# Two-layer attention trunk on one core: a norm row loaded by broadcast, value products moved behind two blocks of filler work, one low part moved to VectorE

## The chip, the cores and the metric

The program runs on one core of a Trainium2 chip. The metric is device time in microseconds (us) of one execution. TensorE (PE) multiplies, VectorE (DVE), ScalarE (ACT) and GpSimd (POOL) do elementwise work, and nearly every DMA is issued by SyncE (SP) on one queue.

## The reference

Two layers over 512 tokens of width 1024, one sequence. Each layer:

```python
h = _rms(x, g_pre)
proj = h @ w_in
o_nsa = _nsa_attention(q_rope, q_nope, k_cmp, v_cmp, k_slc, v_slc, k_win, v_win, nsa_gate)
o_nsa = o_nsa * jax.nn.silu(p_nz)
o_gla = _rms(_gla(gq, gk, gv, log_a), gla_g_norm)
y = m_nsa * (o_nsa @ w_up_nsa) + m_gla * (o_gla @ w_up_gla)
out = y @ w_out
return x + _rms(out, g_post)
```

`_rms(x, g)` is `x * rsqrt(mean(x*x) + 1e-6) * g`. The NSA branch has 8 heads of 64 and adds three attentions (compressed blocks, selected blocks, a window), each with a softmax. With 512 tokens there are only 8 blocks of 64, so selection takes all of them, and both the selected and the window branch are causal attention over all earlier tokens with their own keys and values. The GLA branch is gated linear attention in chunks of 64.

## The kernel before

**Products.** A matrix product in full precision is made of three fp32r products: each operand is split into a high part H (a cast by ACT) and a low part Lo (a subtraction by DVE), and `split3` (lines 175 to 179) multiplies high by high, high by low, low by high. Weights come by DMA into `raw` tiles of which there are three, are split at lines 153 and 154 (or 147 and 148), and are then read by `fm` and `up`. `fm` and `up` are generators that yield after every three products.

**Order of work.** The order of PE's instructions is the order of the program, written by hand. In the first stage (`first_stage`) the order of the other engines is written out as well. Elsewhere a planner puts the instructions of ACT, DVE, POOL and SP in order at compile time, from its own estimates and from each one's place in the program; `tc.high_priority()` raises the instructions inside it. Each engine then runs its list strictly in order.

**First stage.** The x tile of 128 tokens comes in two halves of 512 columns, then A0 (the first weight tile of the first product). The two halves of the row `g_pre` (2 KB each) are loaded into one partition of zeroed tiles, and PE spreads each over 128 partitions by an fp32 product with ones (line 415) into PSUM. `scale_rows` (line 223) multiplies x by the row's factor and by this. `turn_half` transposes on PE, `high` and `low` (lines 241 and 245) make hT, and `prod` multiplies. `keep_busy` issues products on ones that nobody reads.

**Attention.** Heads go in four pairs p. A pair has five steps: m = 0 the compressed branch (`cmp_steps`), m = 1 to 4 `attn_steps` for (ip, br) = (0,0), (0,1), (1,0), (1,1). An attention step has two score units (`scores`: PE product, then DVE maximum at line 970, ACT exponential, DVE scale and transposition), after which SP writes the result to DRAM (line 940) and reads it back in another layout as four DMAs into `PT` (line 943). Its third part, called the values here, multiplies `PT` by v into the pair's accumulator `acc` (line 998). `acc` lies in the only PSUM buffer of tag "o"; the pair's third compressed part opens it (line 918). After a pair's last values, DVE reads it (line 1003, `f_`), ACT makes H (line 1005) and POOL the low part Lo (line 1006).

The loop of lines 1038 to 1061 weaves this: `go(n)` runs the next part of step n and `fill(us)` runs filler products (`fm` and `up` of the rest of the layer) worth that many us. So at m = 3 of pair p, `go(n - 5)` and `go(n - 4)` are the last values of pair p - 1 (ip = 1, both branches), and `go(n - 3)` opens pair p's `acc`:

```python
go(n)
if m == 3:
    go(n - 5)
    go(n - 4)
fill(f4[0])
```

The times of `FILL` for m = 3 are 1.5, 1.2, 1.5 and 1.8. After the loop the first 16 yields of the up products `un0` and `un1` run, then the last pair's last values, and then the rest: `un` multiplies weights by `oTn[0..3]`, which are the (H, Lo) of the four pairs, in `up`.

Of the kernel before, what the change touches and what calls it, by code (L numbers as in the profile page):

```python
# [9 lines left out]
F32 = mybir.dt.float32  # L10
# [4 lines left out]
OP = mybir.AluOpType  # L15
# [52 lines left out]
def trunk(ctx, tc, x, wpk, sp, gvec, cs, wa, out):  # L68
# [243 lines left out]
    for l in range(L):  # L312
# [73 lines left out]
        def first_stage():  # L386


            ones, rows = new("p", dt=BF), [new("p") for _ in range(2)]
            onef = new("p")[:, 0:128]  # L390
            for t in rows:
                V.memset(t, 0.0)
            V.memset(ones, 1.0)
            V.memset(onef, 1.0)
            idle = ps("o")

            def keep_busy(n):
                for _ in range(n):
                    mm(idle, ones[:, 0:128], ones, start=True, stop=True)

            xs = [[new("g") for _ in range(2)]]
            dma(xs[0][0], x[0:128, 0:512])
            nc.scalar.dma_start(xs[0][1], x[0:128, 512:1024])
            issue(0)
            for h in range(2):
                nc.scalar.dma_start(rows[h][0:1], gvec[0, 0:1, h * 512:(h + 1) * 512])
            for i in range(3):
                issue(i)
                xs.append(load_x(x, i + 1, "g"))
            dma(spt, sp[0])  # L410
            shapes = mask_shapes()
            keep_busy(WARM[0])
            gpre = [ps("s") for _ in range(2)]
            for h in range(2):
                mm(gpre[h], onef, rows[h], start=True, stop=True)
            xn = [[new("p") for _ in range(2)] for _ in range(2)]
            q2 = [new("sm", (128, 2), tag="q2") for _ in range(4)]
            xn += xn

            def split_w(n, part):  # L420
                r, w, H, Lo = first_w[n]
                if part:
                    V.tensor_sub(Lo[:, :w], r[:, :w], H[:, :w].bitcast(F32))
                else:
                    A.copy(H[:, :w], r[:, :w])

            acc = [ps("mm") for _ in range(3)]

            def prod(s, n, parts):

                for part in parts:
                    for k in range(n * 3, min(n * 3 + 3, KT)):
                        w = first_w[n][2 + part][:, (k % 3) * 296:(k % 3) * 296 + 296]
                        for t in hTs(k, s)[:2 - part]:
                            mm(acc[s][:, :296], t, w, start=(s, k, 0) not in begun and k == 0 and part == 0,
                               stop=(n == 2 and k == KT - 1 and part == 1))
                            begun.add((s, k, 0))

            begun = set()
            square(q2[0], xs[0], xn[0], 0, A)  # L440
            square(q2[0], xs[0], xn[0], 1, V)
            rs = row_scale(q2[0])
            split_w(0, 0)
            square(q2[1], xs[1], xn[1], 0, A)
            scale_rows(xs[0], xn[0], rs, gpre)
            keep_busy(WARM[1])
            b0 = [turn_half(xn[0], h) for h in range(2)]
            keep_busy(WARM[2])
            for h in range(2):
                high(0, h, b0[h], HT)  # L450
            square(q2[1], xs[1], xn[1], 1, V)
            rs = row_scale(q2[1])
            for h in range(2):
                low(0, h, b0[h], HT)
            split_w(1, 0)
            scale_rows(xs[1], xn[1], rs, gpre)
            prod(0, 0, (0,))
            prod(0, 1, (0,))
            b1 = [turn_half(xn[1], h) for h in range(2)]
            square(q2[2], xs[2], xn[2], 0, A)  # L460
            square(q2[2], xs[2], xn[2], 1, A)
            split_w(2, 0)
            split_w(0, 1)
            rs = row_scale(q2[2])
            for h in range(2):
                high(1, h, b1[h], HT)
                low(1, h, b1[h], HT)
            keep_busy(1)
            prod(0, 2, (0,))
            prod(0, 0, (1,))  # L470
            scale_rows(xs[2], xn[2], rs, gpre)
            for n in range(3):
                prod(1, n, (0,))
            prod(1, 0, (1,))
            b2 = [turn_half(xn[2], h) for h in range(2)]
            square(q2[3], xs[3], xn[3], 0, A)
            square(q2[3], xs[3], xn[3], 1, A)
            split_w(1, 1)
            rs = row_scale(q2[3])
            for h in range(2):  # L480
                high(2, h, b2[h], HT)
                low(2, h, b2[h], HT)
            prod(0, 1, (1,))
            prod(1, 1, (1,))
            scale_rows(xs[3], xn[3], rs, gpre)
            split_w(2, 1)
            drawn = masks(*shapes)
            for n in range(3):
                prod(2, n, (0,))
            for n in range(2):  # L490
                prod(2, n, (1,))
            b3 = [turn_half(xn[3], h) for h in range(2)]
            for h in range(2):
                a = high(3, h, b3[h], HT)
                v = low(3, h, b3[h], HT)
            behind.extend((a.ins, v.ins))
            for s in range(3):
                prod(s, 2, (1,))
                take_A(s, acc[s])
            acc.append(ps("o"))  # L500
            for n in range(3):
                prod(3, n, (0, 1))
            take_A(3, acc[3])
            return drawn
# [226 lines left out]
        def up(f, gate, wn, src, then):  # L731
            th = []

            def sig(o):
                th.append(new("th"))
                A.activation(th[0], o, AF.Tanh, scale=0.5)

            yield from fm(l, f"{gate}{f}", hT, sig)
            w = get(l, f"{wn}{f}")
            u = ps("mm")  # L740
            for k in range(4):
                sl = slice(k * 128, (k + 1) * 128)
                split3(u, (w[0][:, sl], w[1][:, sl]), src[k], k == 0, k == 3)
                if k == 3:
                    then(th[0], u)
                yield 0.64
# [233 lines left out]
        def attn_steps(p, ip, br):  # L980
            for i in (2 * ip, 2 * ip + 1):
                if i or not br:
                    scores(p, i, (br,) if i else (0, 1))
                else:
                    turn(p, br, i, held.pop(p))
                yield

            acc, W = PR[p][3], PT[p, br, ip]
            i0 = 2 * ip
            for j in range(i0 + 2):  # L990
                for g in range(2):
                    c0 = br * 128 + g * 64
                    if j <= i0:
                        m = W[:, :, :2 * (i0 + 1) * 64].rearrange("p a (i j g q) -> p i a j g q", i=2, g=2, q=32)
                        m, w = m[:, :, :, j, g], 256
                    else:
                        m, w = W[:, :, (2 * j) * 64 + g * 32:(2 * j) * 64 + g * 32 + 32], 128
                    mm(acc[g * 64:(g + 1) * 64, (i0 + 2) * 128 - w:(i0 + 2) * 128],  # L998
                       vsw[j // 2][:, j % 2, c0:c0 + 64], m,
                       start=False, stop=(br == 1 and j == i0 + 1), skip_group_check=True)  # L1000
            if ip == 1 and br == 1:
                f_ = new("p")
                V.scalar_tensor_tensor(f_, acc, 0.5, PR[p][2], op0=OP.mult, op1=OP.mult)
                H, Lo = new("oT", dt=F32R), new("oT", dt=F32R)
                A.copy(H, f_)  # L1005
                G.tensor_tensor(Lo, f_, H.bitcast(F32), op=OP.subtract)  # L1006
                oTn[p] = (H, Lo)
            yield

# [28 lines left out]
        for n in range(len(steps)):  # L1038
            m = n % 5
            f4 = FILL[m]  # L1040
            if m == 0:
                need(f"q{steps[n][0]}")
            if m == 4:
                need(f"nz{steps[n][0]}")
            go(n)
            if m == 3:
                go(n - 5)
                go(n - 4)
            fill(f4[0])
            if m == 2:  # L1050
                go(n - 2)
            fill(f4[1])
            if m != 0:
                go(n)
                fill(f4[2])
            if m == 3:
                go(n - 3)
            if m == 4:
                go(n - 3)
                go(n - 2)  # L1060
            fill(f4[3])
        need("ug7")

        uns = [up(f, "mgn", "un", oTn, take_un(f)) for f in range(8)]
# [123 lines left out]
```

## Time and profile before

| | |
|---|---|
| median of 3 runs | 809.79 us (808.65 to 813.39) |
| the profiled execution | 808.68 us |
| its span, first to last instruction | 807.0 us |
| PE busy | 789.5 us (98%) |
| DVE / ACT / POOL busy | 553.5 / 354.4 / 97.6 us |

In the rows an instruction is named by engine, line and operation. "[2.06 <-DMA PT<-tp]" behind a row says that the engine stood idle for 2.06 us before it and that this DMA ended the idle time, and x16 that 16 instructions are taken together. SPq rows are DMAs issued by SP. Busy times of PE are modelled, as matmuls are pipelined: starts are to be trusted more than ends.

### The profile page before, as it was taken

To read this page: it belongs to the slowest core of one execution; us is meant where nothing else is said; L and a number is where in the kernel's file an instruction comes from. 1 tells how busy PE (TensorE), PEld (TensorE's weight loads), DVE (VectorE), ACT (ScalarE), POOL (GpSimd) and SP (SyncE) were. 2 spreads that over 40 slices of the span, in tenths; PEclk is the share of its full clock that TensorE was granted. 3 is DMA by queue.
4 is the path that set the end of the run, shared out by engine and by line. 5 is a ranking of instruction groups with operands and counts; after the bars stand their busy time and mean duration, and the time that the engine had idled before them with its cause. 6 is when DMAs were issued, how large, how long until landed. Compare 5 with 4: busy or idle time off the path is not lost. (4 is left out here: it accounts for less than half of the span.)

```text
span 807.0 us, 12043 instructions
## 1 busy us (share of the span) xinstructions
PE 789.5 (98%) x4262; PEld 644.4 (80%) x4262; DVE 553.5 (69%) x1274; ACT 354.4 (44%) x731; POOL 97.6 (12%) x117
## 2 busy tenths in 40 slices
PE   8999999999989999999999999999999999999996
PEld 5888788887878887888898878888877788788885
DVE  6753749999998945645574366589999987366223
ACT  5671236554554524442356413556555444245211
POOL 3000024000010102211010102311000101032100
PEclk9999999999999999999999999999999999999998
DMA  6641124367676773446246121234767677545222
GB/s 233 229 147 58 53 67 130 105 191 217 183 236 204 235 227 119 153 153 223 79 129 212 52 78 54 83 114 149 223 201 215 214 212 222 171 157 158 78 105 79
DMA packets 54272, 124.04 MB, mean 154 GB/s; under 512 B 6562, under 2 KB 23490, under 8 KB 54212
## 3 DMA queue, kind: packets, MB, share of 16 engines
q1 hardware_dynamic: 54064, 123.01, 48.4%
q8 instruction: 34, 0.56, 0.3%
q10 hardware_dynamic: 148, 0.27, 0.1%
q14 instruction: 26, 0.21, 0.1%
HBM read 94.94 MB, written 25.17 MB: 149 GB/s over the span
## 5 line engine op out<-in xcount | busy, mean ns | idle before, releaser
L177 PE MATMUL ps_mm<-hT,hl 128*128 128x512 f32 x544 | 217.5, 400 | 0.0
L178 PE MATMUL ps_mm<-hT,hl 128*128 128x512 f32 x544 | 212.5, 391 | 0.0
L179 PE MATMUL ps_mm<-hT,hl 128*128 128x512 f32 x544 | 212.3, 390 | 0.0
L153 ACT CAST hl<-raw 128x1024 fp32r<-128x1024 f32 (+3 forms) x107 | 97.6, 915 | 138.3 <-PE ps_mm L178 99.9
L154 DVE TENSOR_TENSOR hl<-raw,hl 128x1024 fp32r<-128x1024 f32 (+3 forms) x107 | 117.4, 1098 | 47.6 <-ACT hl L153 42.5
L177 PEld LDWEIGHTS ps_mm<-hT,hl 128*128 128x128 f32 x544 | 102.2, 188 | 23.3 <-issue 3.1
L179 PEld LDWEIGHTS ps_mm<-hT,hl 128*128 128x128 f32 x544 | 102.2, 188 | 22.1
L178 PEld LDWEIGHTS ps_mm<-hT,hl 128*128 128x128 f32 x544 | 102.4, 188 | 19.0
L972 ACT ACTIVATE g<-g,sx 128x128 f32<-128x128 f32 (+3 forms) x128 | 71.0, 555 | 67.9 <-DVE sx L970 67.5
L935 DVE STREAM_TRANSPOSE T<-g 128x256 f32<-128x256 f32 (+3 forms) x128 | 58.6, 491 | 0.7
L975 DVE TENSOR_SCALAR g<-g,sx,gt 128x128 f32<-128x128 f32 (+3 forms) x128 | 57.0, 459 | 1.5
L178 PE MATMUL ps_mm<-oT,hl 128*128 128x512 f32 x128 | 50.3, 393 | 1.7 <-POOL oT L1006 1.7
L177 PE MATMUL ps_mm<-oT,hl 128*128 128x512 f32 x128 | 50.9, 398 | 0.0
L179 PE MATMUL ps_mm<-oT,hl 128*128 128x512 f32 x128 | 49.9, 390 | 0.0
L1006 POOL TENSOR_TENSOR oT<-p,oT 128x512 fp32r<-128x512 f32 x8 | 14.3, 1784 | 239.0 <-ACT oT L1005 239.0
L998 PE MATMUL ps_o<-PT,a 128*64 128x256 f32 (+1 forms) x384 | 38.6, 348 | 3.9 <-DMA PT<-tp 3.9
L998 PEld LDWEIGHTS ps_o<-PT,a 128*64 128x64 f32 x384 | 25.4, 137 | 18.3 <-issue 9.4
L200 POOL TENSOR_TENSOR rs<-ms,mhalf 128x1 f32<-128x1 f32 (+1 forms) x24 | 17.2, 719 | 177.0 <-DVE ms L198 175.3
L1026 POOL TENSOR_TENSOR p<-p,g 128x512 f32<-128x512 f32 x16 | 28.0, 1750 | 84.3 <-DVE p L1025 72.7
L970 DVE CUSTOM_DVE_ANT_0 g<-ps_t,cmask 128x256 f32<-128x256 f32 (+3 forms) x64 | 28.8, 477 | 2.3 <-PE ps_t L957 2.2
L970 DVE CUSTOM_DVE_ANT_0 g<-ps_s,cmask 128x128 f32<-128x128 f32 (+3 forms) x64 | 29.0, 481 | 1.7 <-PE ps_s L957 1.7
L178 PEld LDWEIGHTS ps_mm<-oT,hl 128*128 128x128 f32 x128 | 24.1, 188 | 6.5 <-POOL oT L1006 2.3
(269 smaller groups left out, 1313.3 us busy)
## 6 DMA issues: line engine op xcount, KB each, us to landing
raw<-wpk SPq DMA_DIRECT2D x96, 512.0 KB, 3.8
tp<-T SPq DMA_DIRECT2D x16, 896.0 KB, 4.1
PT<-tp SPq DMA_DIRECT2D x64, 224.0 KB, 4.9
raw<-wpk SPq DMA_DIRECT2D x32, 256.0 KB, 3.0
tp<-T SPq DMA_DIRECT2D x16, 384.0 KB, 2.5
PT<-tp SPq DMA_DIRECT2D x64, 96.0 KB, 2.4
a<-wpk SPq DMA_DIRECT2D x16, 256.0 KB, 5.7
p<-x SPq DMA_DIRECT2D x16, 256.0 KB, 2.9
```

The costliest lines, as they stand in the source:

```text
L153: A.copy(H[:, :w], r[:, :w])
L154: V.tensor_tensor(Lo[:, :w], r[:, :w], H[:, :w].bitcast(F32), op=OP.subtract)
L177: mm(o, w[0], h[0], start=first, stop=False)
L178: mm(o, w[0], h[1], start=False, stop=False)
L179: mm(o, w[1], h[0], start=False, stop=last)
L200: G.tensor_tensor(r[:, :n], ms[:, :n], mhalf[:, :n], op=OP.pow)
L935: V.transpose(t[:, :, :, g], pps[g][:, :n * 128].rearrange("p (j b q) -> p b j q", j=n, b=4))
L970: V.tensor_tensor_reduce(pp[:, :w], ob, cmask[:, 512 - w:512], 1.0, -3 * NEG, OP.add, OP.min, sx[:, 0:1])
L972: A.activation(pp[:, :w], pp[:, :w], AF.Exp, bias=sx[:, 0:1], scale=-1.0, accum_out=sx[:, 1:2])
L975: V.tensor_scalar(pp[:, :w], pp[:, :w], sx[:, 2:3], gt[:, i, h * 3 + 1 + br:h * 3 + 2 + br], op0=OP.mult, op1=OP.mult)
L998: mm(acc[g * 64:(g + 1) * 64, (i0 + 2) * 128 - w:(i0 + 2) * 128], vsw[j // 2][:, j % 2, c0:c0 + 64], m, start=False, stop=(br == 1 and j = ...
L1026: G.tensor_tensor(t_, t_, y2[f], op=OP.add)
```

## The change

There are four edits. (a) The second half of the first norm row comes by a DMA that reads the row once for each of the 128 partitions, issued by SP right behind the first half of the x tile and ahead of A0; one zeroed tile, one row load and one fp32 product of PE go. (b) `up` multiplies high by high, low weight by high, and then high weight by low. (c) `f_` gets high priority, and the last pair's Lo is made by DVE instead of POOL. (d) At m = 3 the previous pair's last values come behind the first two fillers, and the opening of `acc` behind the fourth.

```diff
-            ones, rows = new("p", dt=BF), [new("p") for _ in range(2)]
+            ones, row = new("p", dt=BF), new("p")
             onef = new("p")[:, 0:128]
-            for t in rows:
-                V.memset(t, 0.0)
+            V.memset(row, 0.0)
...
+            gpre = [ps("s"), new("p")]
             xs = [[new("g") for _ in range(2)]]
             dma(xs[0][0], x[0:128, 0:512])
             nc.scalar.dma_start(xs[0][1], x[0:128, 512:1024])
+            dma(gpre[1], gvec[0, 0, 512:1024].partition_broadcast(128))
             issue(0)
-            for h in range(2):
-                nc.scalar.dma_start(rows[h][0:1], gvec[0, 0:1, h * 512:(h + 1) * 512])
+            nc.scalar.dma_start(row[0:1], gvec[0, 0:1, 0:512])
...
-            gpre = [ps("s") for _ in range(2)]
-            for h in range(2):
-                mm(gpre[h], onef, rows[h], start=True, stop=True)
+            mm(gpre[0], onef, row, start=True, stop=True)
...
-                split3(u, (w[0][:, sl], w[1][:, sl]), src[k], k == 0, k == 3)
+                mm(u, w[0][:, sl], src[k][0], start=(k == 0), stop=False)
+                mm(u, w[1][:, sl], src[k][0], start=False, stop=False)
+                mm(u, w[0][:, sl], src[k][1], start=False, stop=(k == 3))
...
-                V.scalar_tensor_tensor(f_, acc, 0.5, PR[p][2], op0=OP.mult, op1=OP.mult)
+                with tc.high_priority():
+                    V.scalar_tensor_tensor(f_, acc, 0.5, PR[p][2], op0=OP.mult, op1=OP.mult)
                 H, Lo = new("oT", dt=F32R), new("oT", dt=F32R)
                 A.copy(H, f_)
-                G.tensor_tensor(Lo, f_, H.bitcast(F32), op=OP.subtract)
+                (G if p < 3 else V).tensor_tensor(Lo, f_, H.bitcast(F32), op=OP.subtract)
...
             go(n)
-            if m == 3:
-                go(n - 5)
-                go(n - 4)
             fill(f4[0])
             if m == 2:
                 go(n - 2)
             fill(f4[1])
+            if m == 3:
+                go(n - 5)
+                go(n - 4)
             if m != 0:
                 go(n)
                 fill(f4[2])
-            if m == 3:
-                go(n - 3)
             if m == 4:
                 go(n - 3)
                 go(n - 2)
             fill(f4[3])
+            if m == 3:
+                go(n - 3)
```

## Rows read from the trace of the kernel before

**Rows 1.** What PE waited for: us in total, times, longest us.

```profile
PE ps_o L998 <- DMA PT<-tp: 3.9, 2, 2.1
...
PE ps_mm L178 <- POOL oT L1006: 1.7, 2, 0.8
```

**Rows 2.** Timeline, values of two pairs on PE: start us, us, instruction, count.

```profile
228.50 1.73 PE L998 MATMUL ps_o<-PT,a 128*64 128x256 f32 x16
...
232.29 1.74 PE L998 MATMUL ps_o<-PT,a 128*64 128x256 f32 x16 [2.06 <-DMA PT<-tp]
...
267.12 3.25 PE L998 MATMUL ps_o<-PT,a 128*64 128x256 f32 x32
```

**Rows 3.** Timeline, SP's issues ahead of those values.

```profile
219.09 6.20 SPq L136 DMA_DIRECT2D raw<-wpk  x2
225.40 1.80 SPq L943 DMA_DIRECT2D PT<-tp  x4
...
261.87 1.75 SPq L943 DMA_DIRECT2D PT<-tp  x4
```

**Rows 4.** The page's DMA issues: count, KB each, median us from issue to landing.

```profile
PT<-tp SPq DMA_DIRECT2D x64, 224.0 KB, 4.9
```

**Rows 5.** Busy time of PE, PEld, DVE, ACT and POOL during the first layer's attention.

```profile
160.00:290.00 130.00, 127.94 (x690) 102.67 (x689) 119.79 (x357) 64.69 (x162) 8.46 (x5) 1.00 0.68 208
```

**Rows 6.** Timeline, the first pair's last values, its `f_`, and the next opening.

```profile
192.09 3.25 PE L998 MATMUL ps_o<-PT,a 128*64 128x256 f32 x32
...
200.23 0.66 DVE L1003 SCALAR_TENSOR_TENSOR p<-ps_o,oT 128x512 f32<-128x512 f32 x1
...
201.09 0.41 PE L918 MATMUL ps_o<-p,vbd 128*128 128x512 f32 x1
```

**Rows 7.** Timeline, second pair: `f_` after its values.

```profile
235.44 0.65 DVE L1003 SCALAR_TENSOR_TENSOR p<-ps_o,oT 128x512 f32<-128x512 f32 x1
```

**Rows 8.** Timeline around the last pair's `f_`, H and Lo in the first layer.

```profile
305.93 1.29 DVE L148 TENSOR_TENSOR a<-raw,a 128x512 fp32r<-128x512 f32 x2
...
307.13 0.69 DVE L1003 SCALAR_TENSOR_TENSOR p<-ps_o,oT 128x512 f32<-128x512 f32 x1
...
307.55 0.39 PE L179 MATMUL ps_mm<-oT,hl 128*128 128x512 f32 x1
...
308.23 0.39 PE L179 MATMUL ps_mm<-oT,hl 128*128 128x512 f32 x1
...
308.54 1.27 POOL L1006 TENSOR_TENSOR oT<-p,oT 128x512 fp32r<-128x512 f32 x1 [33.40 <-ACT oT L1005]
...
310.21 0.40 PE L179 MATMUL ps_mm<-oT,hl 128*128 128x512 f32 x1
```

**Rows 9.** Timeline of the first stage, up to the second tile's transposition.

```profile
1.70 0.91 SPq L259 DMA_DIRECT2D g<-x  x2
...
4.65 4.11 PE L415 MATMUL ps_s<-p,p 128*128 128x512 f32 x4 [0.16 <-DMA p<-gvec]
...
8.80 0.75 DVE L223 SCALAR_TENSOR_TENSOR p<-g,rs,ps_s 128x512 f32<-128x512 f32 x1 [1.24 <-PE ps_s L415]
...
8.98 1.71 PE L237 MATMUL ps_t<-ident,p 128*128 128x128 f32 x8
...
9.46 0.69 DVE L214 SCALAR_TENSOR_TENSOR p<-g 128x512 f32<-128x512 f32 x1
...
10.70 1.34 DVE L245 TENSOR_TENSOR hT<-ps_t,hT 128x512 fp32r<-128x512 f32 x2
...
13.12 1.03 PE L237 MATMUL ps_t<-ident,p 128*128 128x128 f32 x8
```

**Rows 10.** DMA issues of the whole run, x tiles of the first stage.

```profile
g<-x SPq DMA_DIRECT2D x7, 256.0 KB, 5.7
```

**Rows 11.** DMA of 365 to 368 us, where the later broadcast rows move; packets and rate.

```profile
DMA packets 355, 0.65 MB, mean 216 GB/s; under 512 B 39, under 2 KB 39, under 8 KB 355
```

**Rows 12.** DMA of 6 to 12 us, the first stage's loads.

```profile
DMA packets 1185, 2.31 MB, mean 386 GB/s; under 512 B 133, under 2 KB 247, under 8 KB 1185
```

## Prediction, made before the changed kernel was run

> **What bounds the kernel now.** I read the busy shares by stretch, then the list of what PE waited for, then the timeline around each of its waits. PE is the bound: even in the attention stretch it shows 127.9 of 130 us busy [rows 5]. So only what takes time out of PE's own list counts: its waits, and work that it does while nothing else is ready. Two waits of the list lie where the diff works [rows 1]: two for the transposed weights `PT` (3.9 us together) and two for a low part that POOL makes (1.7 us together). Both come once in each layer. The third place is the start, where PE's list is thin because x, the norm row and the transposes come one after another. DVE is second: 119.8 of 130 us in that stretch [rows 5]. It can be what a moved stall falls on.
>
> **Edit (d), the values.** Second pair, first layer: the first half of the values starts at 228.50, the second at 232.29 after an idle 2.06 us. Where nothing is missing, 32 instructions take 3.25 us, so 16 take 1.63 [rows 2]. The second half should have started at 230.13; it lost 2.16. The list of waits shows two such waits, of 2.1 at the longest and 3.9 in all [rows 1], so the second layer loses about 2.0. Together 4.1 us.
>
> Why late: SP was held from 219.09 to 225.29 by two weight loads that wait for a free `raw` tile, and the four `PT` loads were issued from 225.40 to 227.2 behind them [rows 3]. With the median of 4.9 us to landing [rows 4] and the last issue near 226.8, they land near 231.7; the wait ended at 232.29.
>
> The edit puts the first two fillers (1.5 + 1.2 us by the plan) ahead. A step is planned at 0.64 us and takes 0.68 (third products at 307.55 and 308.23) [rows 8], so they last 2.9 us. The first half then starts at 231.4, the second at 233.0, after the data by 0.7 us or more. The wait is gone, and the fillers, the score product and the rest are the same instructions. Nothing is issued more. The gain is 4.1; its lower bound is 0, if SP's or DVE's list comes out later by as much as the values do.
>
> What is late next? PE is then 2.1 us further ahead of DVE. In the third pair the four loads are issued from 261.87, the last near 263.2, and land near 268.1; the second half of those values starts at 267.12 + 1.63 = 268.75 [rows 2, 3, 4]. That margin of 0.65 becomes 0.65 + 2.9 - 2.1 = 1.4. So nothing is lost there.
>
> The opening of `acc` needs `f_`. In the first pair the values end at 192.09 + 3.25 = 195.34, `f_` starts only at 200.23 and the opening follows at 201.09, right on its heels [rows 6]. In the second pair `f_` follows 1.4 us after the values' 234.03 [rows 2, 7]. After the edit the values end at 198.2 and the opening comes one filler later: 201.09 + 1.9 = 203.0. If `f_` keeps its lag of 4.9 us it ends at 203.8, and PE waits 0.8 once in each layer, 1.6 in all. If high priority gives it the short lag, nothing. I take nothing and keep 1.6 for the range.
>
> **Edits (b) and (c), the last low part.** The third products of a step start 0.68 us apart. That of `un0`'s last step starts at 310.21, after 308.23 [rows 8]: 1.98 instead of 0.68, so 1.3 us are lost, in each of two layers: 2.6. The chain is `f_` at 307.13 (0.69), H by ACT, Lo by POOL from 308.54 to 309.81. `f_` started 0.8 after the values because DVE was at two subtractions (305.93 to 307.22).
>
> With priority `f_` follows the first of them, near 306.6, and ends at 307.3; H is there at 307.95. A DVE subtraction of this shape takes 0.65, half of the 1.29 for two [rows 8], so Lo is there by 308.6, or by 309.2 if the second subtraction comes between. PE would reach that step at 308.46 and, by edit (b), need Lo only as the third operand, at 308.92. So all of 1.3 goes, or 1.0. If DVE has an unrelated subtraction of 1024 columns in front of Lo (as long as two of 512, 1.29), nothing is won. I take 2.6, bounds 0 and 2.6. Elsewhere (b) costs nothing: the number and shape of the products stay, and what `up` waits for is POOL's low part alone [rows 1]. POOL's cover goes, but DVE has room here: its next work is for products that come later.
>
> **Edit (a), the first row.** Two fp32 products hold PE for 4.11 us, one for 2.05. DVE's second scaling waited 1.24 for the second one, so it could start at 7.56 instead of 8.80 [rows 9]. But behind it DVE needs the second x tile: the square at 9.46, from which the low part at 10.70 follows 1.24 later. The second half of that tile was issued near 2.2 and, by a median of 5.7 us [rows 10], came near 7.9. The broadcast writes 256 KB ahead of it in SP's queue. At the 386 GB/s of this stretch [rows 12] that is 0.68 us; at the 216 GB/s of the stretch in which later broadcasts move [rows 11] it is 1.21; were the broadcasts there the slower part of a mix, perhaps at 150 (an estimate), 1.75. The tile comes at 8.6, 9.1 or 9.65, the low part at 9.85, 10.35 or 10.9: a gain of 0.85 or 0.35, or a loss of 0.2. I take PE as dense from there, so that it passes through to the end, and 0.4, near the middle value. A0 is late by as much, but its cast on ACT is not needed until hT's low part is there. The row of zeros not written saves DVE half a microsecond before x has come: nothing.
>
> TensorE's clock speaks against this edit. Eight transposes of the first tile take 1.71 us, the same eight of the second 1.03 [rows 9]: the first ran at the lower level (1.2 GHz) for most of the time, although PE had been working nearly without a break. The edit takes 2.05 us of that work away. If the rise comes 2.05 us later, measured in what follows, as much work runs at half speed and 1.0 us is lost, so that (a) costs 0.6.
> The Trainium skill (TensorE: Matmul & The Clock Gate, Part 1: The HAM clock gate) says that the array starts throttled and that activity releases it; the two times of the transposes agree, and whether this activity is missed no row here tells. By that rule the sum below would be 6.1, without it 7.1.
>
> **Sum.** 4.1 + 2.6 + 0.4 = 7.1 us. The profiled execution took 808.68 (span 807.0 and 1.7 around it), so 801.6 by its own time. The median of the runs is 809.79, 1.1 more; with 7.1 off it, 802.7.
>
> **The rivals.**
> 1. *The clock rises later* (above): 802.7 + 1.0 = 803.7. For it: PE has less to do before 7.6. Against: dummies and transposes still fill most of it.
> 2. *DVE takes the gain of (d) back.* PE gets ahead by 4.1 us over two layers, but DVE at 92% cannot follow; some later score or `PT` is waited for instead, or `f_` is late at 1.6. Then (a), (b) and (c) remain: 809.79 - 3.0 = 806.8. For it: DVE's 119.8 of 130 us. Against: the margin of 1.4 worked out above.
> 3. *Slower: `f_` stands at the head of DVE's list.* The planner may put the prioritised `f_` right behind the score product, ahead of the softmax of those scores, while the values that it needs now come a filler later. DVE, in order, then stands for up to 2.9 + 3.25 = 6.1 us, at six places (three pairs, two layers). DVE's idle 10.2 of 130 us lets it regain about 2.9 in a pair, which takes some 37 us (last values at 192.09 and 228.50) [rows 2, 5, 6]. It decides from a stand of 4.8 us: 6 x (4.8 - 2.9) = 11.4, less 7.1, is over 4 slower. At 5.5 us: 15.6 - 7.1 = 8.5 slower, 818.3. For it: `f_` today is late by 0.8 to 4.9, so priority does move it. Against: a planner that knows when the values end puts it behind them.
>
> **How the numbers follow.** Forecast 0.55 (own range 801 to 805), rival 1 0.15, rival 2 0.20, rival 3 0.10. The first two are faster by more than 0.5%, which is 4 us and about what a measurement of this kernel tells from no change: 0.70. Rival 2 is within: 0.20. Rival 3: 0.10. The likeliest is 802.7. The range begins at 800.5: every term at its better bound makes 7.6, so 802.2, less the 1.1 by which the lowest of the three runs lies under their median, and rounded down. It ends at 808.0, which takes in the single lower bounds, rival 1 and rival 2 with 1.2 above it, and leaves rival 3 out.
>
> **What would show it.** PE's wait for `PT` at line 998 gone in both layers, no new one at the opening of `acc`; `un0`'s last step 0.7 us after the one before; the first tile's low part near 10.3 us instead of 10.70. Wrong if DVE shows an idle time ahead of `f_`, if PE waits for DVE in the score products, or if the x tiles come over 1.2 us later.

## The result and the profile after

The kernel became slower: 819.29 us median of 5 runs (817.28 to 820.91) against 810.1 us for the kernel before in the same session, a ratio of 1.0096 with a 95% interval of 1.0073 to 1.012. That lies outside the range 800.5 to 808.0.

The profiled execution of after, the slowest of the five, has a span of 819.2 us, 12.2 more than that of before. The first view to read is again the list of PE's waits (us in total, times, longest us):

```profile
PE ps_o L998 <- DMA PT<-tp: 7.9, 5, 3.3
```

POOL's low part [rows 1] is gone from it, and so is any wait at the opening of `acc` (line 918). But the wait for `PT`, which was to vanish, has grown from 3.9 to 7.9 us. The timeline of PE in the second pair shows that it is another wait. After first, then the one row of before that stands in the same place:

```profile
210.04 0.87 PE L998 MATMUL ps_o<-PT,a 128*64 128x256 f32 x8
214.12 1.55 PE L998 MATMUL ps_o<-PT,a 128*64 128x256 f32 x8 [3.21 <-DMA PT<-tp]
215.60 0.80 PE L177 MATMUL ps_mm<-hT,hl 128*128 128x512 f32 x1
216.19 0.63 PE L178 MATMUL ps_mm<-hT,hl 128*128 128x512 f32 x1
216.62 0.63 PE L179 MATMUL ps_mm<-hT,hl 128*128 128x512 f32 x1
...
223.73 0.39 PE L177 MATMUL ps_mm<-hT,hl 128*128 128x512 f32 x1
223.96 0.39 PE L178 MATMUL ps_mm<-hT,hl 128*128 128x512 f32 x1
...
240.15 3.25 PE L998 MATMUL ps_o<-PT,a 128*64 128x256 f32 x32
```

```profile
208.78 1.52 PE L998 MATMUL ps_o<-PT,a 128*64 128x256 f32 x16
```

The last values of the pair, which waited 2.06 us in their middle [rows 2], now run as one block of 32 from 240.15: edit (d) did what it says. The wait sits a block earlier, at the second half of the pair's *first* values (m = 4), which in before ran as one block, and it lasts 3.2 us. Behind it the products start 0.43 us apart (216.19, 216.62) and from 223.3 on 0.23 apart again. The clock says why. The windows give busy time of PE, PEld, DVE, ACT and POOL, the granted clock, the DMA share and GB/s:

```profile
205.00:210.00 5.00, 5.00 (x24) 3.99 (x22) 4.26 (x12) 2.85 (x9) 0.79 (x1) 1.00 0.32 75
210.00:213.00 3.00, 0.92 (x9) 0.49 (x8) 2.90 (x8) 2.95 (x6) 0.00 (x0) 1.00 0.96 297
213.00:215.00 2.00, 0.88 (x5) 0.58 (x6) 1.94 (x7) 0.70 (x3) 0.00 (x0) 0.50 0.99 411
215.00:220.00 5.00, 5.00 (x21) 3.86 (x18) 2.64 (x7) 0.49 (x2) 0.00 (x0) 0.50 0.53 147
220.00:224.00 4.00, 4.00 (x13) 3.10 (x12) 2.81 (x8) 0.42 (x1) 0.00 (x0) 0.59 0.82 240
224.00:230.00 6.00, 6.00 (x32) 5.09 (x31) 4.37 (x22) 3.71 (x11) 0.00 (x0) 1.00 0.48 168
```

From 213 on, while PE stands, the granted clock is 0.50 (1.2 GHz), and it is back at 1.00 (2.4 GHz) only near 223. PE shows as fully busy from 215 to 220, so the share of busy time hides the loss: the same products start nearly twice as far apart.

What held `PT` is in SP's timeline. First after, then before:

```profile
203.21 0.34 SPq L940 DMA_DIRECT2D tp<-T  x1
203.59 5.33 SPq L136 DMA_DIRECT2D raw<-wpk  x2
209.03 1.79 SPq L943 DMA_DIRECT2D PT<-tp  x4
```

```profile
200.34 0.34 SPq L940 DMA_DIRECT2D tp<-T  x1
202.05 0.35 SPq L136 DMA_DIRECT2D raw<-wpk  x1
202.69 1.74 SPq L943 DMA_DIRECT2D PT<-tp  x4
207.01 0.34 SPq L940 DMA_DIRECT2D tp<-T  x1
207.58 8.00 SPq L136 DMA_DIRECT2D raw<-wpk  x2
```

Before, one weight load stood between the write of `tp` and the four `PT` loads. After, two do. The second one (of the weight `mgg3`) has to wait for a `raw` tile. That tile becomes free when DVE has made a low part, which is no earlier than before:

```profile
207.92 0.65 DVE L154 TENSOR_TENSOR hl<-raw,hl 128x512 fp32r<-128x512 f32 x1
```

So SP stands until 208.6, and the `PT` loads go out at 209.03 instead of 202.69. Not all of this is the stand: after is 1.3 us behind from the first stage, and `tp` is written 2.9 us later in all. Nor does edit (d) move any DMA past another in the program. It is the planner's list that differs: five loads in each layer stand one place earlier, in front of the `PT` loads of a unit. Fillers that come earlier need their weights earlier, which fits, but no trace shows the planner's reasons. DVE's and ACT's lists differ at a few places too, so that SP's order is one of several candidates until it is tested by itself.

Matching PE's filler products of the two profiled executions one by one gives the 12.2 us (after minus before, us):

| place | layer 0 | layer 1 |
|---|---|---|
| first stage | +1.36 | |
| second pair's first values: wait and lower clock | +7.55 | +6.67 |
| second pair's last values: the old wait gone | -2.25 | -2.06 |
| third and fourth pair's first values: small new waits | +1.27 | +1.34 |
| last low part, at `un0`'s last step | -0.85 | -0.85 |

### The profile page after: what moved, and what is told of

The parts are those of the page before. It is cut to its first block, busy times and chain, and to the rows that moved or that the text cites. A ratio compares the mean times of both kernels' runs of the same rounds, so it can differ in the third digit from the quotient of the medians.

```text
span 819.2 us, 12027 instructions
## 1 busy us (share of the span) xinstructions
PE 797.3 (97%) x4260; PEld 650.3 (79%) x4260; DVE 554.9 (68%) x1275; ACT 353.3 (43%) x731; POOL 90.9 (11%) x115
## 5 line engine op out<-in xcount | busy, mean ns | idle before, releaser
L177 PEld LDWEIGHTS ps_mm<-hT,hl 128*128 128x128 f32 x544 | 103.5, 190 | 23.4 <-issue 2.9
L179 PEld LDWEIGHTS ps_mm<-hT,hl 128*128 128x128 f32 x544 | 103.3, 190 | 22.7
L178 PEld LDWEIGHTS ps_mm<-hT,hl 128*128 128x128 f32 x544 | 103.6, 190 | 19.3
L1007 POOL TENSOR_TENSOR oT<-p,oT 128x512 fp32r<-128x512 f32 x6 | 7.8, 1297 | 188.9 <-ACT oT L1006 188.9
```

What stands on the lines that cost most here:

```text
L177: mm(o, w[0], h[0], start=first, stop=False)
L178: mm(o, w[0], h[1], start=False, stop=False)
L179: mm(o, w[1], h[0], start=False, stop=last)
```

## The experiments

All times are medians; each ratio is to runs of the kernel before on the same chip (808.02 to 814.27, medians 810.1 to 811.1). The ratios differ by up to 0.002 from the quotient of the two medians, so gains taken as differences of medians are rough to 1 or 2 us.

### One edit at a time

Edit (a) alone has the lines of the first stage, edits (b) and (c) have `up`, the priority of `f_` and the last Lo, and edit (d) alone is the loop, without that priority:

```diff
             go(n)
-            if m == 3:
-                go(n - 5)
-                go(n - 4)
             fill(f4[0])
...
             fill(f4[1])
+            if m == 3:
+                go(n - 5)
+                go(n - 4)
...
-            if m == 3:
-                go(n - 3)
...
             fill(f4[3])
+            if m == 3:
+                go(n - 3)
```

**Edit (a).** 

> Edit (a) alone. Theory 1 (the broadcast delays the x tiles behind it, PE goes idle ahead of its first products and its clock falls): PE reaches the products after the first stage 1.3 us later than before, so +1.3 us, some 811.4 against 810.1; the second half of the second x tile comes 1.4 us later, and the first twelve products run at the lower level. Rival (the 1.3 us of the changed kernel came from its other edits): no change or the 0.4 us gain that was forecast, 809.7.

Measured: 810.98, ratio 1.0003 (0.9986 to 1.002). The first row's edit shows no effect. The interval, from 1.1 us faster to 1.6 us slower, holds both the gain of 0.4 that was forecast and the loss of 1.3.

**Edit (d).** 

> Edit (d) alone, without the priority of f_. Theory 1 (SP's list: a second weight load stands ahead of the second pair's PT loads and holds them): the wait of over 3 us at the second pair's first values and the fall of the clock behind it are there, the wait at the last values is gone; some 12 us over the kernel before, 822. Theory 2 (the prioritised f_ stands in DVE's list): without priority the wait is not there and (d) brings the 4.1 us that were forecast, 806.

Measured: 818.97, ratio 1.0095 (1.008 to 1.011). The whole loss comes from (d), and without the priority. It is 7.7 us (0.0095 x 811.11) where theory 1 had 12. Its PE waits for `PT` are 8.8 us in 6 places, and SP has the same two weight loads ahead of the `PT` loads (200.90 for 5.33 us, then 206.34).

**Edits (b) and (c).** 

> Edits (b) and (c) alone. Theory 1: SP's list is that of before, so the wait for PT at the last values stays at 2 us a layer, no new one appears, and un0's last step loses 0.4 us instead of 1.3: 1.7 us faster, 808.4. Theory 2 (priority of f_ delays the softmax on DVE): a new wait for PT, 3 us or more slower.

Measured: 808.44, ratio 0.9965 (0.9951 to 0.998): a gain of 2.8 us (0.0035 x 811.11), interval 1.6 to 4.0. POOL's wait is gone and that for `PT` stays, 4.4 us, as theory 1 had it.

### SP's order put back

The weight loads that had moved ahead are put behind a `PT` load that they overtook; the rest is the changed kernel. `turned` lists the `PT` loads as they are issued.

```diff
+HELD = {"mgg3": 3, "ug5": 4, "mgg6": 3, "un0": 4, "mgn1": 3}
...
-        dma(r[:, :w], src)
+        with tc.issue_after(turned[-HELD[n]]) if n in HELD else nullcontext():
+            dma(r[:, :w], src)
```

**All edits, five loads held.** 

> All edits, with five weight loads in each layer held behind the PT loads that they overtook, so that SP's list in the attention stretch is that of the kernel before. Theory 1: the second pair's first values find their PT and PE's clock stays up; the wait at the last values stays gone: +1.3 (first row) - 4.1 (values) - 1.7 (last low part) = 4.5 faster than before, 805.6. Rival (DVE is too far behind, so PT comes late whatever SP does): the wait of 3 us stays and the time is 815 or more.

Measured: 803.01, ratio 0.9894 (0.9878 to 0.9911). No wait for `PT` is left in PE's list. It is 2.6 us under theory 1: the profiled execution lost 0.4 us in the first stage and not 1.3, and before's median holds falls of the clock behind the old wait, which are gone here (see edit (d) alone, below). SP's list of loads is again that of before, row by row, but for the one load of edit (a):

```profile
202.29 0.34 SPq L942 DMA_DIRECT2D tp<-T  x1
202.68 0.43 SPq L138 DMA_DIRECT2D raw<-wpk  x1
204.86 1.74 SPq L945 DMA_DIRECT2D PT<-tp  x4
```

So 16.3 us (819.29 - 803.01) hang on the place of five DMAs a layer in one queue. The lists of PE, ACT and POOL are those of after, and DVE's too but for one transposition a layer, so what else the planner changed with (d) is not the cause.

**The same without (a).** The first stage is that of before.

> The last kernel (weight loads held) without edit (a). If (a) is worth nothing, as its run alone says: the same time, 803.0, within 0.2%. If it brings the forecast 0.4: 803.4. If it costs the 1.3 us by which the profiled execution of the changed kernel lay behind after the first stage: 801.7.

Measured: 802.16, ratio 0.9903 (0.9885 to 0.992), which the run with (a) can't be told from, so that the three expectations can't be told apart either. It is the lowest median of all kernels here.

**Only the first of the five held**: `HELD = {"mgg3": 3}`.

> The changed kernel with one weight load in each layer (the gate weights number 3) held behind the second pair's PT loads; the later pairs keep the changed list. Theory 1: this one load is the cause of the wait of 3.2 us and of the fall of the clock: both go, and only the waits of some 0.6 us at the third and fourth pair stay: 805.4. Rival (the later overtakings cost as much): 810 or more.

Measured: 811.29, ratio 1.0014 (0.9999 to 1.0028). The expectation missed: the wait didn't go, it moved to the third pair's first values.

```profile
244.58 0.87 PE L1001 MATMUL ps_o<-PT,a 128*64 128x256 f32 x8
248.07 0.87 PE L1001 MATMUL ps_o<-PT,a 128*64 128x256 f32 x8 [2.62 <-DMA PT<-tp]
248.87 0.79 PE L179 MATMUL ps_mm<-hT,hl 128*128 128x512 f32 x1
249.46 0.63 PE L180 MATMUL ps_mm<-hT,hl 128*128 128x512 f32 x1
249.89 0.63 PE L181 MATMUL ps_mm<-hT,hl 128*128 128x512 f32 x1
```

Behind the wait the products again start 0.43 us apart. Its SP shows the next overtakings. A second weight load stands in front of the `PT` loads at 236.27, and one that waits for a tile until 242.25 in front of those at 242.73, whose landing ends the wait:

```profile
229.94 6.22 SPq L138 DMA_DIRECT2D raw<-wpk  x2
236.27 1.79 SPq L945 DMA_DIRECT2D PT<-tp  x4
...
242.27 0.35 SPq L138 DMA_DIRECT2D raw<-wpk  x1
242.73 1.79 SPq L945 DMA_DIRECT2D PT<-tp  x4
```

In after these overtakings cost only some 0.6 us each. A reading that fits both is that the first stall had put PE so far back there that the later loads were nearly in time: with the first mended, the next comes out.

**Every weight load behind the `PT` loads**, with edits (b) and (c) and the loop of before:

```diff
-        dma(r[:, :w], src)
+        with tc.issue_after(last_back[-1]) if last_back else nullcontext():
+            dma(r[:, :w], src)
```

> Edits (b) and (c) and the loop of the kernel before, (d) not made; instead every weight load is issued behind the PT loads that the program has named before it. Theory 1 (PT was late already in the kernel before because weight loads held SP): the wait of 2.1 us at the second pair's last values goes and the time is that of the held kernel, 803 to 804. Rival (DVE delivers the scores too late, or the weights now come too late): the wait stays, or products wait for weights: 808 or more.

Measured: 915.37, ratio 1.1305 (1.128 to 1.133). Theory 1 missed and the rival's second half holds: PE has no wait for `PT`, but it waits for weights:

```profile
PE ps_mm L178 <- ACT hl L154: 52.6, 12, 7.2
PE ps_mm L744 <- ACT hl L154: 16.1, 10, 2.2
```

Here neither kind of load may always go first in this queue.

### What the clock costs

**The new wait filled.** The changed kernel, with products on constants that nobody reads between the two halves of the second pair's first values. SP's list is that of after.

```diff
             if m == 4:
                 go(n - 3)
+                if n == 9:
+                    idle = ps("mm")
+                    for _ in range(15):
+                        mm(idle, ident_b, cmask, start=True, stop=True)
                 go(n - 2)
```

> The changed kernel, all edits and SP's list as they are, but between the two halves of the second pair's first values TensorE does 15 products on constants that nobody reads, some 3.3 us, about as long as it waits there. Theory 1 (two prices: the wait of 3.2 us, and as much again or more because PE's clock falls in it and stays at the lower level for 7 to 10 us): the wait is filled, PE is no earlier, but the clock stays up, and about 7.8 us come back over the two layers: 811.5. Rival (the wait itself is the price): 819, or 3 us more for each layer if the products come on top of the wait.

Measured: 812.23, ratio 1.0029 (1.0018 to 1.004). `PT` comes just as late, and the products fill the time:

```profile
208.76 0.87 PE L999 MATMUL ps_o<-PT,a 128*64 128x256 f32 x8
209.57 3.41 PE L1063 MATMUL ps_mm<-cmask,ident_b 128*128 128x512 bf16 x15
212.91 0.87 PE L999 MATMUL ps_o<-PT,a 128*64 128x256 f32 x8
```

PE does more than in after and is 7.1 us faster (819.29 - 812.23; 5.4 by the two ratios). The granted clock is 1.00 in all the windows from 205 to 230. By matched products the two executions differ by 4.15 us at this place in layer 0 and by 3.2 in layer 1. This part of the loss is the clock.

**The old wait filled.** Edits (b) and (c) with the loop of before, and ten such products between the second pair's two *last* values (`n == 13`, at m = 3).

> Edits (b) and (c) with the loop of before, and ten products on constants that nobody reads (2.3 us) in each layer between the second pair's two last value steps, where PE waits 2.1 to 2.4 us for PT. Theory, that this old wait lets the clock fall in some executions (its trace in the kernel with (b) and (c) alone shows 0.67 for 233 to 236 us): PE no longer idles there by more than 0.4 us, the clock stays at the upper level, and the 808.4 of the kernel with (b) and (c) alone becomes 805.0 to 807.0 with a spread under 1.5. Rival, that the old wait costs its own length and nothing else: the products only take the place of the wait, 808 to 809.5.

Measured: 806.72 (805.83 to 807.65), ratio 0.9948 (0.993 to 0.9967), where the kernel without them had 0.9965 (0.9951 to 0.998) and a scatter from 806.19 to 810.51. The value is the theory's, but the two intervals overlap; the scatter of 1.8 us is narrower, though not under 1.5, and 0.5 us of waiting stays in layer 1. The traces are clearer: by matched products the filled kernel gains 1.65 us at this place in layer 0 and 0.7 in layer 1 on the unfilled one, whose clock fell there, though its `PT` comes no earlier.

**Edit (d) alone, loads held.** The loop of (d) and the five held loads; first stage, `up` and the low part as before.

> Edit (d) alone, with five weight loads a layer held behind the PT loads so that SP's list in the attention is that of before. Theory (the two waits of 4.1 us, and the falls of the clock behind them, in some executions up to 1.7 us a layer): 811.0 - 4.1 - 0 to 3.4 = 803.5 to 806.9, likeliest 805. Rival, the two waits alone, as the prediction had it: 806.9 or a little above. Second rival, that the values come out no earlier than their data once POOL makes the last low part: 809 to 811.

Measured: 803.23 (802.89 to 804.66), ratio 0.9908 (0.9887 to 0.9928): a gain of 5.8 to 9.2 us (0.0072 to 0.0113 x 810.44). The two waits alone (4.1) lie outside it, and 803.23 is a little under the theory's 803.5. By matched products this execution gains 2.25 and 2.05 us on that of before at the second pair's last values, 4.3 in all, and nothing elsewhere in the attention. It is also 0.9 us ahead after the first stage, whose instructions are the same. What the medians show beyond that fits the clock: before's profiled execution was one in which it held, and where the clock fell behind that wait this cost 1.6 and 2.0 us more (edit (a) alone, by matched products). In 47 executions of the kernel before, timed in this study, the mean granted clock goes with the time: ten at 0.998 have a median of 809.0 us, thirteen at 0.993 one of 811.7.

## Why the prediction was wrong

**Where it failed: edit (d), "Nothing is issued more".** The prediction counted the moved fillers as the same instructions, took SP's list as given although a planner writes it, and looked at SP only for the values that it moved and for the third pair's last ones. It did name the condition, "if SP's or DVE's list comes out later by as much as the values do", but priced it as a gain of 0, and no rival carried it on to a loss. Each filler also issues its weights' loads, on the queue that the `PT` loads share. [rows 3] show two weight loads holding SP for 6.2 us ahead of `PT` loads: the price stood in these rows. The question to ask was which other `PT` loads such a pair would now stand before. It is the pair's first values, where before had one load and no wait.

**The second part was a price.** A wait of PE was costed at its length. The new ones, 3.2 and 3.3 us, cost 7.55 and 6.67 us by matched products, since the clock fell behind them. With the waits filled 4.15 and 3.2 us of this come back, so 3.4 and 3.45 are left, about the length of the waits. The 17.9 us between the profiled executions of after and of the kernel with held loads are these two places (14.3), the small waits at the third and fourth pair (2.6) and the first stage (0.9).

**Without that flaw** the forecast sum of 7.1 would stand, 802.7. All edits with the loads held ran at 803.01. This agreement is partly luck, as the terms show:

- Edit (d): forecast 4.1, measured 4.3 by matched products, and 5.8 to 9.2 over the runs, because the old wait too lets the clock fall in some executions, a price that the prediction had not.
- Edits (b) and (c): forecast 2.6, 1.3 a layer; by matched products 0.85 in each layer, 1.7 in all; 2.8 (1.6 to 4.0) over the runs. The step at `un0` still waits 0.4 us for Lo, now made by DVE:

```profile
314.77 0.39 PE L743 MATMUL ps_mm<-oT,hl 128*128 128x512 f32 x1
315.04 0.68 DVE L1004 SCALAR_TENSOR_TENSOR p<-ps_o,oT 128x512 f32<-128x512 f32 x1
...
316.15 0.39 PE L743 MATMUL ps_mm<-oT,hl 128*128 128x512 f32 x1
316.41 0.69 DVE L1007 TENSOR_TENSOR oT<-p,oT 128x512 fp32r<-128x512 f32 x1 [0.69 <-ACT oT L1006]
...
317.16 0.50 PE L743 MATMUL ps_mm<-oT,hl 128*128 128x512 f32 x1
```

  These two third products are 1.01 us apart; it was 1.98 [rows 8]. The prediction had `f_` jump ahead by priority. It starts 0.8 us after the values (311.02 + 3.25 = 314.27), as before. The priority moved nothing: DVE's list in edit (d) alone, without it, is that of after instruction for instruction, but for the first stage and the added Lo, and so it is for the held kernels with and without it.
- Edit (a): forecast 0.4, measured none (1.0003, 0.9986 to 1.002). The broadcast was mis-sized. The second x tile came at 9.5, against the 9.1 taken, and A0's cast began at 8.28 instead of 5.56. ACT runs its list in order, so that hT's high part stands behind this cast, and "its cast on ACT is not needed until hT's low part is there" missed that. PE then waits 1.0 us for the high part, for which it did not wait before:

```profile
8.28 0.93 ACT L423 CAST hl<-raw 128x888 fp32r<-128x888 f32 x1 [3.37 <-DMA raw<-wpk]
...
9.53 0.69 DVE L214 SCALAR_TENSOR_TENSOR p<-g 128x512 f32<-128x512 f32 x1 [1.48 <-DMA g<-x]
...
9.74 1.05 ACT L241 CAST hT<-ps_t 128x512 fp32r<-128x512 f32 x2
...
10.36 0.40 PE L433 MATMUL ps_mm<-hl,hT 128*128 128x296 f32 x1 [1.03 <-ACT hT L241]
...
10.61 1.28 DVE L245 TENSOR_TENSOR hT<-ps_t,hT 128x512 fp32r<-128x512 f32 x2
```

  hT's low part came at 10.61, against the 10.35 foreseen and 10.70 before [rows 9].

**The opening of `acc`** was right: `f_` follows the first pair's values (196.15 + 3.25) by 3.7 us, at 203.11, and the opening at 204.45 does not wait. That lag lies between the two that were considered, and no run has a wait at the opening.

**The rivals.** Rival 1 (a later rise of the clock in the first stage): after's profiled execution has a clock of 0.62 from 12 to 16 us and stands 1.36 us behind before there. The four other kernels with (a) show 1.00 in that stretch, with (a) alone no loss is clear of the noise, and with the loads held the kernel is as fast with (a) as without. But the first filler product of the first layer starts at 62.4 to 63.7 us in the five traces with (a) and at 60.95 to 62.8 in the seven without it. So a loss of up to about 1 us is neither shown nor excluded. Rival 2 (DVE takes the gain back): the held kernels keep it. Rival 3 (slower by `f_` at the head of DVE's list): the sign was right and the mechanism wrong, since the priority is not needed for the loss (edit (d) alone, 1.0095). That its 818.3 lies near the 819.29 is luck.

What stays open: why the clock stayed down for 10 us in one layer and some 7 in the other, why the planner put the loads earlier, and what (a) is worth.

## What to carry to other kernels

When work is moved past other work and a planner orders the queues, write down the whole list of each queue as it comes out before and after, and look for every load that changes places with another, not only for the ones whose wait is to be removed. A load that waits for a free buffer holds all that stand behind it; here it cost 5.3 us of the queue at once, and holding it back behind the urgent loads, place by place, turned a loss of 8 to 9 us into a gain of about as much. In a kernel like this one, price a wait of TensorE of 2 to 3 us in a dense stretch at about twice its length until the granted clock behind it is read, and where a wait of some us can't be removed, products on constants can make it cheaper, as they did here for the waits of 2.4 and 3.2 us behind which the clock fell.

## What the runs showed of the hardware

**The clock falls for a short wait, and not always.** Idle times of 3.2 and 2.6 us in an otherwise dense stretch were followed by a granted clock of 0.50, for about 10 us in the one case (213 to 223) and some 3 in the other (from 248.8). Behind the old wait of about 2 us either came. In the first layer it lasted 2.06 us in before and 2.08 with edit (a) alone, between the same instructions. First before, then (a) alone:

```profile
233.00:236.00 3.00, 3.00 (x21) 2.35 (x18) 2.97 (x8) 1.05 (x1) 0.00 (x0) 1.00 0.55 165
```

```profile
232.48 2.84 PE L996 MATMUL ps_o<-PT,a 128*64 128x256 f32 x16 [2.08 <-DMA PT<-tp]
...
233.00:236.00 3.00, 3.00 (x16) 2.09 (x13) 2.97 (x8) 0.00 (x0) 0.00 (x0) 0.50 0.61 163
```

It also fell in the kernel with edits (b) and (c) alone, where that wait was 2.43 us:

```profile
229.00:233.00 4.00, 1.57 (x10) 1.13 (x10) 3.54 (x13) 1.31 (x4) 0.00 (x0) 0.82 0.88 287
233.00:236.00 3.00, 3.00 (x16) 2.10 (x14) 2.16 (x7) 0.42 (x1) 0.00 (x0) 0.67 0.74 247
```

In that kernel's second layer it fell behind 1.95 us (0.58 from 627 to 630), so the length alone does not decide. What does isn't shown.

The Trainium skill (TensorE: Matmul & The Clock Gate, HAM oscillation — how this bites in real kernels) tells of a kernel in which TensorE's products wait for a DMA tile after tile, some 3 to 5 us each time, and the clock falls in each of these waits. The traces agree that a wait for a DMA can do it, and here single ones of 1.95 to 3.3 us did; the 2.06 us of [rows 2], after which the clock held, is a wait for a DMA too.

**What a row broadcast to 128 partitions does to the loads behind it in the queue.** The 256 KB of edit (a) made A0's cast start 2.7 us later (8.28 against 5.56; 8.35 with edit (a) alone), where 0.7 to 1.75 had been estimated from the rates of [rows 11, 12]. The second half of the second x tile landed 1.45 us later (9.51 against 8.06), which is inside that estimate. Why A0 lost more isn't shown.
